# A hybrid retention and RG-LRU layer on one core: the recurrence output's last blocks as a pair, norm sums from PSUM, transfers ranked by issue

## The chip, the core and the metric

The kernel runs on one core of a Trainium2 chip. Its time is the device time of one execution in microseconds; three executions of the kernel before gave 1575.84, 1577.02 and 1579.26, median 1577.02 us.

## The reference

One layer of a streaming encoder, batch 1, 1024 tokens (T), width 1024 (D), feed-forward width 3072, everything in fp32:

```python
h = rms_norm(x, norm1_w)
q, k, v, g_ret, x_lru, y_lru, gate_ret, gate_lru = split(h @ w_in)
y_a = (group_norm(retention(rotary(q), rotary(k), v)) * silu(g_ret)) @ w_ret_o
y_b = (rg_lru(conv4(x_lru)) * gelu(y_lru)) @ w_lru_o
mix = sigmoid(gate_ret + b0) * y_a + sigmoid(gate_lru + b1) * y_b
x = x + mix @ w_out
h = rms_norm(x, norm2_w)
gate, val = split(h @ w_up)
x = x + (gelu(conv3(gate)) * val) @ w_dn
return rms_norm(x, norm_f_w)
```

## The kernel before

**Matmuls.** Each operand tile (128x512, fp32) is split into a high and a low part: ScalarE casts the high part (L471), VectorE subtracts it from the source for the low part (L472). A product is the sum of three matmuls, high by high, high by low, low by high. On top of that a large matmul is done in jobs of a 2x2 block scheme with seven products where eight would be plain: `A11, S1, S2, A12, S3, A22, S4` (PRODS). Each needs its own stationary block (a sum of weight blocks, held in `w` tiles; sums at L557 to L566) and its own set of moving tiles (B11, T1, T2, B21, T3, T4, B22, held in `u` tiles). T1 to T4 are sums of blocks of the operand: T1 = B12 - B11, T2 = B22 - T1, T3 = B12 - B22, T4 = B21 - T2. A product is 12 matmuls of 128x512 into one PSUM bank (L720).

**Banks.** A job uses three banks, X, Y and Z, of a pool of six (`g`); a second pool of two (`a`) serves transposes and small sums. A11, S2, S3 and A22 follow each other in bank X, and after each of the first three ScalarE copies the bank to an SBUF tile (L769). The next product of that bank adds to it and so waits for the copy. VectorE makes the job's four results from the copies and the banks (L743, L749, L771).

**Order of the work.** TensorE's order is the order in which `mm_fast` (from L694) issues products. Two jobs that are mates run product by product: A11 of one, A11 of the other, S1 of one, and so on. A job without a mate runs its seven products in a row, except that A11 of the next job is put between its S3 and its A22 (`ahead` in `run`). The other engines' orders come from a planner (`Plan`): the program is first drafted; `latest` goes through it backwards and gives each instruction the latest time by which it should start, taking from each engine's heap the entry of the latest due time; `forward` goes through it forwards and always takes the ready instruction with the earliest such time. `landing` is the planner's own figure for how long a transfer takes. The program is then built a second time in the planned order, and each engine executes its list in order.

**Transfers.** All large DMAs but those of the feed-forward activations are issued from one queue (SP), with eight semaphores in turn, so that a DMA waits for the one that had its semaphore before.

**The stages.** Input projection with the two branches; four jobs for the retention output (w_ro, as pairs 0+1 and 2+3); four jobs for the recurrence output (w_lo: a pair 0+1, then 2 and 3 alone); four jobs for w_out (0 and 1 a pair, 2 and 3 alone); 24 jobs up, 12 down; a final norm.

The results of a recurrence output job are multiplied by their gate (L1418), added to the retention part (L1419) and written to a DRAM buffer `mix_d` (L1421). A w_out job uses `mix` as its stationary blocks: when all the parts that a block needs are written, it is read back (L523), and then cast and summed. The moving operand of w_out, `wop`, is the weight itself: its blocks are loaded from `w_out` (L1761), its sums T1 to T4, made long before, from `tw_d` (L1374). The builder of that operand is posted by `out_start` after one of the recurrence output jobs.

After w_out, each result's squares are summed on ScalarE (L1701). `norm_half` scales the rows by the reciprocal root, and transposes them on TensorE into `a` banks (L1742); for each of the eight blocks of a half it takes the high part (ScalarE, L1747), the low part (VectorE, L1748) and a plain copy (ScalarE, L1751), and releases the bank. Blocks B12, which are needed in sums only, get just the copy. In the second half the order is B22, then B12. `set_by_set` (L861 to L881) then makes T1 to T4 for the up jobs, with the sums L863, L867, L871 and L876.

Of the kernel before, what the change touches and what calls it, by code (L numbers as in the profile page):

```python
# [15 lines left out]
AF = mybir.ActivationFunctionType  # L16
ALU = mybir.AluOpType
# [70 lines left out]
LATE, SOONER = 6, 1  # L88
# [5 lines left out]
class Units:  # L94
# [25 lines left out]
    def put(self, *tiles, late=LATE):  # L120
        for t in tiles:
            self.count += 1
            heapq.heappush(self.q, (self.now[0] + late, self.count, self.at.pop(id(t))[0]))
# [76 lines left out]
class Plan:  # L200
# [54 lines left out]

    def landing(self, s):
        if s.bytes <= 4096:
            return 1950.0
        return (self.READ if s.read else self.WRITE) + s.bytes * self.MOVE

    def latest(self, pe):

        todo = {n: len(a) for n, a in self.after.items()}
        due = dict.fromkeys(self.steps, 0.0)
        free = dict.fromkeys(self.ENGINES, 0.0)
        heaps = {e: [] for e in self.ENGINES}
        start, left, open_pe = {}, len(self.steps), set()
        pe = list(pe)

        def ready(n):  # L270
            s = self.steps[n]
            if s.eng == "PE":
                open_pe.add(n)
            else:
                heapq.heappush(heaps[s.eng], (-due[n], n))

        def end(n):
            s = self.steps[n]
            return min(free[s.eng], due[n] - (self.landing(s) if s.dma else s.tail))

        for n, k in todo.items():
            if not k:
                ready(n)
        while left:
            best = None
            for e in self.ENGINES:
                if e == "PE":
                    n = pe[-1] if pe and pe[-1] in open_pe else None
                else:
                    n = heaps[e][0][1] if heaps[e] else None  # L290
                if n is not None and (best is None or end(n) > best[0]):
                    best = end(n), e, n
            t, e, n = best
            pe.pop() if e == "PE" else heapq.heappop(heaps[e])
            s = self.steps[n]
            start[n] = free[e] = t - s.hold
            left -= 1
            for a in self.before[n]:
                p = self.steps[a]
                lag = self.lag(p, s, False)  # L300
                due[a] = min(due[a], start[n] + 1e6 if lag is None else start[n] - lag)
                todo[a] -= 1
                if not todo[a]:
                    ready(a)
        return start
# [122 lines left out]
def tile_trunk_layer(ctx, tc, x, xt, positions, params, consts, normf, w_in, w_v, w_ro, w_lo,  # L428
# [39 lines left out]
    def split(src, get=get):  # L468

        hi, lo = get(F32R), get(F32R)  # L470
        S.copy(hi, src)  # L471
        V.tensor_sub(lo, src, hi.bitcast(F32))  # L472
        return hi, lo
# [346 lines left out]
    def pair_src(w, i):  # L820
        return lambda m, kh: w[i, 2 * m + kh]
# [38 lines left out]

    def set_by_set(op, b):  # L861
        for j in range(4):
            V.tensor_sub(b["B11", j], b["B12", j], b["B11", j])  # L863
            op["T1", j] = split(b["B11", j])
            yield 1.2
        for j in range(4):
            V.tensor_sub(b["B11", j], b["B22", j], b["B11", j])  # L867
            op["T2", j] = split(b["B11", j])
            yield 1.2
        for j in range(4):  # L870
            V.tensor_sub(b["B12", j], b["B12", j], b["B22", j])  # L871
            op["T3", j] = split(b["B12", j])
            put(b["B12", j], b["B22", j], late=SOONER)
            yield 1.2
        for j in range(4):
            V.tensor_sub(b["B21", j], b["B21", j], b["B11", j])  # L876
            op["T4", j] = split(b["B21", j])
            put(b["B21", j], b["B11", j], late=SOONER)
            yield 1.2
# [782 lines left out]
        ojobs.append(Job(pair_src(w_ro, n), og, emit_ret_o(n), u_start if n == 1 else None, fast=True, last=n == 3,  # L1662
                         mate=n in (0, 2), fetch=from_sg(0, n), rate=RO_RATE))
    for n in range(4):
        ojobs.append(Job(pair_src(w_lo, n), u, emit_lru_o(n), fast=True, last=n == 3, mate=n == 0,
                         fetch=from_sg_t1(n)))
    jobs += ojobs
    warmth = get()
# [50 lines left out]
    def norm_half(half):  # L1719
# [18 lines left out]
        for k in (range(KT), (4, 5, 6, 7, 0, 1, 2, 3))[half]:  # L1738
            ps = psa.get()
            for t in range(4):  # L1740
                c0 = 128 * (k % 4)
                PE.transpose(ps[:, 128 * t:128 * t + 128], z[t, k // 4][:, c0:c0 + 128], ident)  # L1742
            w = pc("norm2_w", k)
            key = f"B{k // 4 + 1}{half + 1}", k % 4
            if key[0] != "B12":
                hi, lo = get(F32R), get(F32R)
                S.activation(hi, ps, AF.Copy, scale=w)  # L1747
                V.scalar_tensor_tensor(lo, ps, w, hi.bitcast(F32), ALU.mult, ALU.subtract)  # L1748
                h2[key] = (hi, lo)
            f = keep2[key] = get()  # L1750
            S.activation(f, ps, AF.Copy, scale=w)  # L1751
            psa.put(ps)
            yield (0.5, 0.25)[half]
        put(*z.values())
# [9 lines left out]
    def out_start():  # L1764
# [4 lines left out]
                 pre=((0, 0), (0, 1), (1, 1)), fetch=from_x(t), mate=t == 0, prods=FIRST if t < 2 else PRODS,  # L1769
                 ready=lambda m, kh, t=t: all((4 * kh + j, t // 2) in mixed for j in range(4)))  # L1770
             for t in range(4)]
    ojobs[-2].post = out_start
    queue.extend(wjobs)

    run(jobs)
# [257 lines left out]
```

## Time and profile before

| what | value |
|---|---|
| median of three runs | 1577.02 us (1575.84 to 1579.26) |
| profiled execution, its own time | 1576.54 us |
| its span in the profile | 1574.8 us |
| granted TensorE clock, mean | 0.999 |
| TensorE busy | 1561.6 us, 99% of the span |
| VectorE busy | 1382.9 us, 88% |
| ScalarE busy | 954.1 us, 61% |
| DMA, whole span | 281.07 MB, mean 178 GB/s |
| matmuls, of which L720 | 7061, 6060 |

The span is what the profile records between the first and the last instruction; the execution's own time is 1.7 us longer. PE is TensorE's matmuls, ACT ScalarE, DVE VectorE, SP the queue that issues transfers. Where an engine is busy for 99% of the span, the interesting rows are those of its idle time: which instruction came late, and what ended the wait. A row of a timeline ends with that in brackets.

### The profile page before, as it was taken

Reading aid. Unit: us, or ns where it says so; the run is one execution under the profiler, and the core shown is the slowest. Engines: PE = TensorE matmul, PEld = TensorE weight load, DVE = VectorE, ACT = ScalarE, POOL = GpSimd, SP = SyncE. Lnnn points to the kernel's source line nnn. Section 1 sums busy time; section 2 is a strip of 40 time slices with the busy share of each in tenths; the row PEclk is TensorE's granted clock in tenths of the full one; section 3 lists DMA queues with packets and bytes.
Section 4 is the critical chain, followed back from the end, with each engine's and each line's share of the span. In section 5 each row is a group of like instructions: output and inputs, shape, how many; then the busy total and the mean of one; then the engine's idle time right before and its main releaser. Section 6 shows DMA issues by size and latency. Waiting matters only on the chain.

```text
span 1574.8 us, 21660 instructions
## 1 busy us (share of the span) xinstructions
PE 1561.6 (99%) x7061; PEld 1289.4 (82%) x7061; DVE 1382.9 (88%) x2472; ACT 954.1 (61%) x1655; POOL 63.3 (4%) x81
## 2 busy tenths in 40 slices
PE   9999999999999999999999999999999999999998
PEld 7888888888878888888878888888888888888887
DVE  8999988988989998999998899777777778987885
ACT  7547966656558797855365764444444446563653
POOL 0001000000000000000000001000000000000000
PEclk9999999999999999999999999999999999999999
DMA  9344333454364346684997246444444466787752
GB/s 313 110 134 146 127 126 115 137 193 143 112 205 141 114 140 189 224 278 156 309 336 241 86 134 208 138 144 140 135 140 138 138 192 223 261 277 268 262 181 85
DMA packets 158865, 281.07 MB, mean 178 GB/s; under 512 B 17304, under 2 KB 29728, under 8 KB 158752
## 3 DMA queue, kind: packets, MB, share of 16 engines
q1 hardware_dynamic: 152944, 263.43, 51.2%
q0 software_dynamic: 4224, 13.64, 2.9%
q10 hardware_dynamic: 1584, 2.63, 0.5%
q8 instruction: 55, 0.90, 0.2%
q14 instruction: 58, 0.48, 0.1%
HBM read 194.68 MB, written 83.89 MB: 177 GB/s over the span
## 4 chain that ended last, share of the span: by engine, by line
PE 45%; DVE 4%; DMA 2%; issue 1%; ACT 1%; SPq 0%; POOLq 0%; DVEq 0%; ACTq 0%
PE g L720 44%; DVE w L472 1%; DVE u L472 1%; DMA mix_d<-u 1%; DVE u L1419 0%; PE a L1742 0%; DMA u<-sg_d 0%; DMA w<-mix_d 0%; DMA x_d<-u 0%; DVE u L749 0%; DVE u L1418 0%; DMA u<-x 0%; DMA u<-w_out 0%; DVE w L560 0%; DVE w L563 0%
## 5 line engine op out<-in xcount | busy, mean ns | idle before, releaser
L720 PE MATMUL g<-u,w 128*128 128x512 f32 x6060 | 1414.7, 391 | 4.1 <-ACT u L769 2.5
L720 PEld LDWEIGHTS g<-u,w 128*128 128x128 f32 x6060 | 1129.2, 188 | 236.0 <-ACT u L769 4.5
L471 ACT CAST w<-w 128x512 fp32r<-128x512 f32 x519 | 317.9, 621 | 324.1 <-PE g L720 222.6
L472 DVE TENSOR_TENSOR w<-w,w 128x512 fp32r<-128x512 f32 x519 | 351.7, 683 | 54.4 <-ACT w L471 49.2
L749 DVE TENSOR_TENSOR u<-g,u 128x512 f32<-128x512 f32 x216 | 147.3, 684 | 45.8 <-PE g L720 35.4
L471 ACT CAST u<-u 128x512 fp32r<-128x512 f32 x253 | 150.3, 620 | 55.2 <-PE g L720 5.3
L769 ACT COPY u<-g 128x512 f32<-128x512 f32 x218 | 126.8, 582 | 79.8 <-PE g L720 72.9
L472 DVE TENSOR_TENSOR u<-u,u 128x512 fp32r<-128x512 f32 x253 | 166.4, 682 | 1.4 <-ACT u L471 1.2
L1789 DVE SCALAR_TENSOR_TENSOR u<-u,par,u 128x511 f32<-128x511 f32 (+1 forms) x96 | 71.3, 745 | 2.9 <-ACT u L1786 2.6
L1472 PE MATMUL g<-w,u 128*128 128x512 f32 x264 | 61.9, 390 | 0.2
L1472 PEld LDWEIGHTS g<-w,u 128*128 128x128 f32 x264 | 49.3, 188 | 11.6 <-issue 0.7
L557 DVE TENSOR_TENSOR w<-w,w 128x512 f32<-128x512 f32 x72 | 49.2, 684 | 6.1 <-DMA w<-ff_d 2.2
L1794 POOL DMA_DIRECT2D ff_d<-u x48 | 36.1, 753 | 450.3 <-DVE u L1793 450.3
L1124 PE MATMUL a<-u,u 128*128 128x512 f32 x192 | 50.8, 391 | 0.1
L560 DVE TENSOR_TENSOR w<-w,w 128x512 f32<-128x512 f32 x72 | 49.2, 684 | 0.8
L563 DVE TENSOR_TENSOR w<-w,w 128x512 f32<-128x512 f32 x72 | 49.1, 683 | 0.2
L566 DVE TENSOR_TENSOR w<-w,w 128x512 f32<-128x512 f32 x72 | 49.1, 682 | 0.1
L1786 ACT ACTIVATE u<-u,par 128x512 f32<-128x512 f32 x48 | 39.2, 818 | 15.1 <-DVE u L749 14.6
L743 DVE TENSOR_TENSOR u<-u,u 128x512 f32<-128x512 f32 x48 | 32.6, 686 | 16.8 <-ACT u L769 15.9
L1124 PEld LDWEIGHTS a<-u,u 128*128 128x128 f32 x192 | 35.6, 188 | 8.8 <-ACT u L471 0.8
L1793 DVE TENSOR_TENSOR u<-u,u 128x512 f32<-128x512 f32 x48 | 32.9, 687 | 6.0 <-ACT u L1792 5.8
L1106 DVE SCALAR_TENSOR_TENSOR u<-u,par,u 128x511 f32<-128x511 f32 (+2 forms) x48 | 35.7, 743 | 0.7 <-ACT u L1102 0.6
(207 smaller groups left out, 1114.8 us busy)
## 6 DMA issues: line engine op xcount, KB each, us to landing
w<-w_in SPq DMA_DIRECT2D x96, 256.0 KB, 2.8
w<-w_up SPq DMA_DIRECT2D x96, 256.0 KB, 2.8
u<-w_dn SPq DMA_DIRECT2D x84, 256.0 KB, 3.6
u<-x_d SPq DMA_DIRECT2D x60, 256.0 KB, 4.5
x_d<-u SPq DMA_DIRECT2D x48, 256.0 KB, 3.8
ff_d<-u POOLq DMA_DIRECT2D x48, 256.0 KB, 2.7
td_d<-u SPq DMA_DIRECT2D x48, 256.0 KB, 2.8
u<-td_d SPq DMA_DIRECT2D x48, 256.0 KB, 4.6
```

The lines of the kernel that those rows point to most:

```text
L471: S.copy(hi, src)
L472: V.tensor_sub(lo, src, hi.bitcast(F32))
L557: V.tensor_add(s, r["A21"], r["A22"])
L560: V.tensor_sub(s, s, r["A11"])
L563: V.tensor_sub(s, r["A12"], s)
L566: V.tensor_sub(src, r["A21"], r["A11"])
L720: PE.matmul(bank[:, s], w[a][:, c], need(op, (SETS[nm], j))[b][:, s], start=first and n == 0, stop=n == 11, skip_group_check=True)
L749: V.tensor_add(u, bank, u)
L769: S.copy(u, bank)
L1124: PE.matmul(ps, wg[g][a][:, cs], xs[k][b], start=q == 0, stop=q == 5)
L1472: PE.matmul(bank, o[p][:, c], w[q], start=first and j == n == 0, stop=j == 3 and n == 2, skip_group_check=True)
L1789: V.scalar_tensor_tensor(c[:, s:], src[:, :TH - s], w, c[:, s:], ALU.mult, ALU.add)
```

## The change

Six edits. (1) Recurrence output jobs 2 and 3 become mates, so that the last half of that output runs as a pair, product by product. (2) `out_start`, and with it the loads of the w_out operand, is posted by the third from last of the eight output jobs (`ojobs[-3]`, recurrence block 1), not by the second from last (block 2). (3) For the blocks B12 of the norm, VectorE makes B12 - B11 and B12 - B22 straight from the PSUM bank, scaled by the norm's weight; ScalarE's copy of these blocks goes, and so do the two subtractions of `set_by_set`. (4) There B22 is released after T2. (5) The planner's figure for transfers of up to 4096 bytes goes from 1950 to 4000. (6) The planner's backward pass takes from a heap the entry with the latest due time for its issue: the due time less the transfer's landing, or less an instruction's tail.

```diff
     def landing(self, s):
         if s.bytes <= 4096:
-            return 1950.0
+            return 4000.0
...
-                heapq.heappush(heaps[s.eng], (-due[n], n))
+                heapq.heappush(heaps[s.eng], (-due[n] + (self.landing(s) if s.dma else s.tail), n))
...
     def set_by_set(op, b):
         for j in range(4):
-            V.tensor_sub(b["B11", j], b["B12", j], b["B11", j])
             op["T1", j] = split(b["B11", j])
             yield 1.2
         for j in range(4):
             V.tensor_sub(b["B11", j], b["B22", j], b["B11", j])
             op["T2", j] = split(b["B11", j])
+            put(b["B22", j], late=SOONER)
             yield 1.2
         for j in range(4):
-            V.tensor_sub(b["B12", j], b["B12", j], b["B22", j])
             op["T3", j] = split(b["B12", j])
-            put(b["B12", j], b["B22", j], late=SOONER)
+            put(b["B12", j], late=SOONER)
             yield 1.2
...
-        ojobs.append(Job(pair_src(w_lo, n), u, emit_lru_o(n), fast=True, last=n == 3, mate=n == 0,
+        ojobs.append(Job(pair_src(w_lo, n), u, emit_lru_o(n), fast=True, last=n == 3, mate=n in (0, 2),
...
             f = keep2[key] = get()
-            S.activation(f, ps, AF.Copy, scale=w)
+            if key[0] != "B12":
+                S.activation(f, ps, AF.Copy, scale=w)
+            else:
+                b11, b22 = keep2["B11", key[1]], keep2["B22", key[1]]
+                V.scalar_tensor_tensor(b11, ps, w, b11, ALU.mult, ALU.subtract)
+                V.scalar_tensor_tensor(f, ps, w, b22, ALU.mult, ALU.subtract)
             psa.put(ps)
...
-    ojobs[-2].post = out_start
+    ojobs[-3].post = out_start
```

**TensorE, the last job of the recurrence output.** Before: the end of S3 of job 3 (bank g_223), seven matmuls of A11 of w_out's first job (bank g_231), and the first matmuls of A22 of job 3.

```order
L720 MATMUL g_223_8000<-u_1380_7528,w_1331_7990 128x512
L720 MATMUL g_223_8000<-u_1379_7527,w_1332_7991 128x512
L720 MATMUL g_231_8322<-u_1522_8149,w_1351_8061 128x512
L720 MATMUL g_231_8322<-u_1523_8150,w_1351_8061 128x512
L720 MATMUL g_231_8322<-u_1522_8149,w_1352_8062 128x512
L720 MATMUL g_231_8322<-u_1526_8155,w_1351_8061 128x512
L720 MATMUL g_231_8322<-u_1527_8156,w_1351_8061 128x512
L720 MATMUL g_231_8322<-u_1526_8155,w_1352_8062 128x512
L720 MATMUL g_231_8322<-u_1530_8161,w_1351_8061 128x512
L720 MATMUL g_223_8000<-u_1382_7532,w_1338_8015 128x512
L720 MATMUL g_223_8000<-u_1383_7533,w_1338_8015 128x512
```

Now: the end of S3 of job 3 (bank g_220) and the beginning of A22 of job 2 (bank g_219), whose S3 is the twelve matmuls ahead of these of g_220.

```order
L720 MATMUL g_220_7899<-u_1379_7527,w_1321_7968 128x512
L720 MATMUL g_220_7899<-u_1380_7528,w_1321_7968 128x512
L720 MATMUL g_220_7899<-u_1379_7527,w_1322_7969 128x512
L720 MATMUL g_219_7878<-u_1382_7532,w_1325_7972 128x512
L720 MATMUL g_219_7878<-u_1383_7533,w_1325_7972 128x512
L720 MATMUL g_219_7878<-u_1382_7532,w_1326_7973 128x512
```

A product of the mate now stands between a bank's S3 and A22 (12 matmuls, and 36 between S2 and S3, where 12 were). From the end of job 3's A22 to the first matmul of A12 of w_out's first job there are now 72 matmuls, before 53.

**VectorE, the last gate product that w_out's first job waits for.** Before: L1418 with bank g_223 and the sum L1419, rows 1377 and 1378 of VectorE's list, behind five splits (L472) of the w_out operand; the list is shown from row 1371.

```order
L749 TENSOR_TENSOR u_1567_8217<-g_226_8069,u_1567_8217 128x512
L472 TENSOR_TENSOR u_1582_8240<-u_1525_8153,u_1581_8239 128x512
L472 TENSOR_TENSOR u_1586_8246<-u_1529_8159,u_1585_8245 128x512
L472 TENSOR_TENSOR u_1590_8252<-u_1533_8165,u_1589_8251 128x512
L472 TENSOR_TENSOR u_1612_8301<-u_1558_8203,u_1611_8300 128x512
L472 TENSOR_TENSOR u_1616_8307<-u_1562_8209,u_1615_8306 128x512
L1418 TENSOR_TENSOR u_1545_8183<-g_223_8000,u_1545_8183 128x512
L1419 TENSOR_TENSOR u_1544_8181<-u_1544_8181,u_1545_8183 128x512
```

Now, from row 1366 (the new lines put L1418 and L1419 at L1417 and L1418): the same for job 2 (bank g_219), then job 3 (bank g_220).

```order
L1417 TENSOR_TENSOR u_1548_8134<-g_219_7878,u_1548_8134 128x512
L472 TENSOR_TENSOR w_1367_8223<-w_1365_8220,w_1366_8222 128x512
L1418 TENSOR_TENSOR u_1547_8132<-u_1547_8132,u_1548_8134 128x512
L472 TENSOR_TENSOR u_1538_8119<-u_1470_7926,u_1537_8118 128x512
L472 TENSOR_TENSOR u_1551_8155<-u_1487_7986,u_1550_8154 128x512
L1417 TENSOR_TENSOR u_1562_8172<-g_220_7899,u_1562_8172 128x512
L1418 TENSOR_TENSOR u_1561_8170<-u_1561_8170,u_1562_8172 128x512
L472 TENSOR_TENSOR u_1632_8331<-u_1571_8192,u_1631_8330 128x512
```

The last gate product and its sum have moved from rows 1377 and 1378 to 1371 and 1372; two splits of the w_out operand, not five, stand just ahead of them.

**ScalarE and VectorE, the last blocks of the norm and the start of the up jobs.** Before, on ScalarE, rows 989 to 999: the four copies L1751 of B12 (from banks a_391 to a_397) between copies of product banks (L769) and casts of the first T1 tiles (L471).

```order
L1747 ACTIVATE u_1838_9243<-a_389_9238,par 128x512
L1751 ACTIVATE u_1837_9236<-a_387_9227,par 128x512
L1751 ACTIVATE u_1840_9247<-a_389_9238,par 128x512
L1751 ACTIVATE u_1842_9274<-a_391_9269,par 128x512
L769 COPY u_1860_9364<-g_261_9327 128x512
L1751 ACTIVATE u_1843_9281<-a_393_9276,par 128x512
L471 CAST u_1854_9350<-u_1756_8991 128x512
L1751 ACTIVATE u_1844_9288<-a_395_9283,par 128x512
L769 COPY u_1865_9397<-g_262_9366 128x512
L1751 ACTIVATE u_1845_9295<-a_397_9290,par 128x512
L471 CAST u_1856_9355<-u_1759_9002 128x512
```

Now, on VectorE, rows 1525 to 1534: the sums L1754 (B12 - B11, into B11's tile) and L1755 (B12 - B22) from the same four banks, in place of L863 and L871.

```order
L1754 SCALAR_TENSOR_TENSOR u_1756_8991<-a_391_9269,par,u_1756_8991 128x512
L566 TENSOR_TENSOR w_1491_8829<-w_1524_9023,w_1491_8829 128x512
L1754 SCALAR_TENSOR_TENSOR u_1759_9002<-a_393_9277,par,u_1759_9002 128x512
L1755 SCALAR_TENSOR_TENSOR u_1842_9274<-a_391_9269,par,u_1831_9214 128x512
L1755 SCALAR_TENSOR_TENSOR u_1843_9282<-a_393_9277,par,u_1834_9225 128x512
L472 TENSOR_TENSOR u_1855_9354<-u_1756_8991,u_1854_9353 128x512
L472 TENSOR_TENSOR u_1857_9358<-u_1759_9002,u_1856_9357 128x512
L1754 SCALAR_TENSOR_TENSOR u_1772_9042<-a_395_9285,par,u_1772_9042 128x512
L1754 SCALAR_TENSOR_TENSOR u_1775_9053<-a_397_9293,par,u_1775_9053 128x512
L866 TENSOR_TENSOR u_1756_8991<-u_1831_9214,u_1756_8991 128x512
```

The four copies are gone from ScalarE's list, and a bank is now read twice by VectorE; for the last two banks (a_395, a_397) the second read, L1755, is at rows 1545 and 1546.

## The prediction

> **What bounds the kernel now.** I read the page's head first, then TensorE's waits, then the timelines of the engines around each wait, and the chain last.
>
> ```profile
> span 1574.8 us, 21660 instructions
> PE 1561.6 (99%) x7061; PEld 1289.4 (82%) x7061; DVE 1382.9 (88%) x2472; ACT 954.1 (61%) x1655; POOL 63.3 (4%) x81
> PE g L720 <- ACT u L769: 2.5, 4, 1.3
> PE g L720 <- ACT w L471: 1.3, 1, 1.3
> PE a L1742 <- ACT a L1701: 0.5, 1, 0.5
> PE g L720 <- ACT u L471: 0.3, 1, 0.3
> 900.57 664.90 PE g L720 x2932
> ```
>
> TensorE (PE) is busy for 99% of the span, and the change leaves its matmuls as they are, in number and shape. The last row, from the chain of waits, says that from 900.57 us on they run without a gap: 664.90/2932 = 0.2268 us each. So time is to be had only from PE's waits ahead of 900, which the rows above it list (total, times, longest). They total some 5 us: a few tenths of a per cent of the span are all that this change can win. PE's timeline shows where they stand (start, length, count, in brackets the idle time before the row and what ended it):
>
> ```profile
> 764.61 20.11 PE L720 MATMUL g<-u,w 128*128 128x512 f32 x88
> 785.45 4.62 PE L720 MATMUL g<-u,w 128*128 128x512 f32 x19 [0.72 <-ACT u L769]
> 791.40 15.03 PE L720 MATMUL g<-u,w 128*128 128x512 f32 x65 [1.33 <-ACT u L769]
> 807.70 17.53 PE L720 MATMUL g<-u,w 128*128 128x512 f32 x75 [1.28 <-ACT w L471]
> 857.00 0.66 PE L1742 MATMUL a<-cst,u 128*128 128x128 f32 x4 [0.48 <-ACT a L1701]
> 898.44 1.88 PE L720 MATMUL g<-u,w 128*128 128x512 f32 x7 [0.25 <-ACT u L769]
> 900.57 11.63 PE L720 MATMUL g<-u,w 128*128 128x512 f32 x50 [0.26 <-ACT u L471]
> ```
>
> A row's length holds 0.16 us in which the next matmul could already run (88 x 0.2268 = 19.96, the row says 20.11), so each wait costs its idle time and 0.16: **0.88, 1.49 and 1.44** in the last half of the recurrence output and at the start of w_out, then 0.64, 0.41 and 0.42 around the norm. Six waits, 5.3 us.
>
> The first two are waits for the copy of bank X (L769). ScalarE's own timeline shows why the copy is late:
>
> ```profile
> 783.59 0.62 ACT L471 CAST u<-u 128x512 fp32r<-128x512 f32 x1 [1.55 <-DMA u<-w_out]
> 784.29 0.62 ACT L471 CAST w<-w 128x512 fp32r<-128x512 f32 x1
> 784.81 0.58 ACT L769 COPY u<-g 128x512 f32<-128x512 f32 x1
> ...
> 789.61 1.25 ACT L471 CAST u<-u 128x512 fp32r<-128x512 f32 x2 [0.63 <-DMA u<-tw_d]
> 790.76 0.58 ACT L769 COPY u<-g 128x512 f32<-128x512 f32 x1
> 780.00:810.00 30.00, 26.67 (x114) 20.82 (x113) 27.87 (x46) 20.51 (x37) 0.00 (x0) 1.00 1.06 376
> ```
>
> Both copies stand in ScalarE's order behind casts of the w_out operand, which wait for their transfers. The last row (busy time of PE, weight loads, DVE, ACT, POOL; then clock, DMA share, GB/s) shows the DMA engines full at 1.06 and VectorE 27.87 of 30 us busy: here everything but PE is short. The third wait is the chain:
>
> ```profile
> 795.35 0.68 DVE L1418 TENSOR_TENSOR u<-g,u 128x512 f32<-128x512 f32 x1
> 796.06 0.70 DVE u L1419
> 796.78 4.80 DMA mix_d<-u
> 801.65 0.32 SPq L523
> 802.49 5.21 DMA w<-mix_d
> 807.72 0.63 ACT w L471
> ```
>
> The last tile that w_out's first job needs is gated (L1418, L1419), written to DRAM, read back as a stationary block, cast. From the write's issue to the first matmul of that product (A12 of job 0) it takes 807.70 - 796.78 = 10.92 us.
>
> **The change, part by part.** *The pair.* The diff makes recurrence output blocks 2 and 3 a pair. Before, the single job had 7 matmuls between S3 and A22 of one bank, 7 x 0.2268 = 1.59 us for a copy that takes 0.58 and stands behind others; between S2 and S3 there were 12. Now 12 of the mate stand between S3 and A22 (2.72 us) and 36 between S2 and S3 (8.2 us). Both waits were at most 1.49 with the shorter cover. The S2-S3 one is then covered by 24 further matmuls (5.4 us), the S3-A22 one by 5 more (1.13 us): 0.88 and 1.49 go, though the copies of the pair still stand behind casts of the w_out operand in ScalarE's order. Value -2.37, ends 0 (both return, below) and -2.37.
>
> What is late next is the chain. Without the two waits PE would be at job 0's A12 at 807.70 - 1.44 - 2.37 = 803.89; the last A22 moves from 53 to 72 matmuls ahead of it, 19 x 0.2268 = 4.3 us earlier, and is through at about 803.89 - 72 x 0.2268 = 787.6. But VectorE does not come to it then, being full:
>
> ```profile
> 791.74 0.68 DVE L749 TENSOR_TENSOR u<-g,u 128x512 f32<-128x512 f32 x1
> 792.34 3.09 DVE L472 TENSOR_TENSOR u<-u,u 128x512 fp32r<-128x512 f32 x5
> ```
>
> In VectorE's order of the changed kernel the last gate product and sum are rows 1371 and 1372, before 1377 and 1378; the rows that had these six places were the one at 791.74 and the five from 792.34. So the sum ends near 793.0 and the write goes at about 793.1. Plus 10.92: 804.0 against 803.89, a wait of 0.1. With a busier DMA queue, and VectorE ahead or behind by two instructions (0.60 us from start to start in its row of five: 3.09 = 4 x 0.60 + 0.69), I hold 0 to 1.5 possible and take 0.6. So the third wait shrinks by 0.84.
>
> *The norm's sums.* Four copies L1751 and the subtractions L863 and L871 (4 each) go; eight VectorE sums straight from PSUM come.
>
> ```profile
> L1751 ACT ACTIVATE u<-a,par 128x512 f32<-128x512 f32 x16 | 10.9, 691 | 2.3 <-DVE u L1748 2.0 <-PE a L1742 0.3
> L863 DVE TENSOR_TENSOR u<-u,u 128x512 f32<-128x512 f32 x4 | 2.7, 686 | 1.8 <-ACT u L1751 1.8
> L1748 DVE SCALAR_TENSOR_TENSOR u<-a,par,u 128x512 fp32r<-128x512 f32 x12 | 8.8, 746 | 1.6 <-ACT u L1747 1.6
> 896.11 0.70 ACT L1751 ACTIVATE u<-a,par 128x512 f32<-128x512 f32 x1
> 896.69 0.63 ACT L471 CAST u<-u 128x512 fp32r<-128x512 f32 x1
> 897.20 0.70 ACT L1751 ACTIVATE u<-a,par 128x512 f32<-128x512 f32 x1
> 897.78 0.60 ACT L769 COPY u<-g 128x512 f32<-128x512 f32 x1
> ```
>
> A VectorE sum of this kind costs 746 ns (L1748 has the same operands) against 686 for what it replaces: 8 x 0.06 = 0.5 us more on VectorE. Four of them stand ahead of the first T1 split, where three subtractions stood: 0.60 + 4 x 0.06 = 0.84 us later in VectorE's order. That is hidden, since the L863 row shows 1.8 us of idle time ahead of these subtractions, waiting for the copies L1751 that the sums no longer need. ScalarE loses 4 x 0.69 = 2.8 us, and it was back to back there: the copy that ended the wait at 898.44 stood behind three of them, and the cast that ended the one at 900.57 behind the last. Both waits (0.41 + 0.42) go; what can come instead is a wait of the last two transposes for their PSUM bank, which is now held by two VectorE sums (1.5 us) rather than one 0.69 copy. I take 0.2 for that: -0.63, ends -0.83 and +0.8 (two banks, 1.49 - 0.69 = 0.8 each, less 0.83).
>
> [...]
>
> ```profile
> L749 DVE TENSOR_TENSOR u<-g,u 128x512 f32<-128x512 f32 x216 | 147.3, 684 | 45.8 <-PE g L720 35.4 <-ACT u L769 10.1
> L743 DVE TENSOR_TENSOR u<-u,u 128x512 f32<-128x512 f32 x48 | 32.6, 686 | 16.8 <-ACT u L769 15.9 <-DMA u<-x 0.7
> ```
>
> [...]
>
> *Transfers ranked by issue, small ones due earlier, the operand started one job earlier.* These cost no instruction but one more ACT table load. They reorder each engine before about 900 us: PE's rows move by at most 30 places, on average by under 3. From the third up job on all engines' orders are the same as before, so nothing happens after 900.57. PE had waits of about 2.2 us in total before 700; reordering may remove some or add as many.
>
> ```profile
> L1147 ACT ACT_TABLE_LOAD x13 | 16.7, 1283 | 0.2
> 150.00:460.00 310.00, 309.44 (x1523) 258.89 (x1522) 283.46 (x583) 206.07 (x390) 11.30 (x8) 1.00 0.43 140
> ```
>
> The table load (1.28 us) falls where ScalarE has a third of its time free (206 of 310 us busy). I take 0, ends -1 and +1.5 (a table load that no idle time covers).
>
> Sum: -2.37 - 0.84 - 0.63 + 0 = **-3.84 us**. The profiled execution took 1576.54 (its span is 1574.8), so 1572.7; the median of the three runs stands 0.48 above the profiled one: **1573.2**.
>
> **The rivals.** *The waits only move.* If the last sum does not come earlier (VectorE as late as 796.06, since its order there is set by splits whose casts wait for transfers), PE arrives at A12 at 803.89 and waits until 807.70, 3.8 us: the gain of the pair is nil, and -0.63 remains: 1576.4. For it speaks the full DMA queue (1.06); against it the six places in VectorE's order, and that the first w_out load stands ten places earlier in SP's.
>
> *Slower.* The loads of the w_out operand now start a job earlier, and two splits of that operand stand just ahead of the last gate product in VectorE's row (1369, 1370). If their transfers are late, the product waits behind them in order, and with it the write, the read and A12. To come out 3.15 us above the median of before, the wait at A12 must be 3.15 + 3.81 + 0.63 = 7.6 us, the write at 800.6, 7.5 later than I put it. One that is at 801 gives 1580.6. Against it: the longest transfer on the chain in this stretch is below, and those loads are issued ten or more places before.
>
> ```profile
> 780.11 5.49 DMA mix_d<-u
> ```
>
> *Reordering.* Keys that rank transfers by issue might expose a wait in the projections or the values stage: +1.3 where one table load comes onto the path and up to +3 where two such delays coincide, or the 2.2 us of old waits go: 1571.0 to 1576.2.
>
> **How the numbers follow.** A difference under 0.2% (3.15 us) can't be told from none in this kernel. The sum lies 0.7 us beyond that bound, so the chances split: forecast 0.62 (0.46 of it faster, 0.16 within), waits only move 0.18 (0.17 within, 0.01 slower), slower by late loads 0.10, reordering 0.10 (half faster, half within). Together faster 0.51, same 0.38, slower 0.11. The range: low by the residual wait gone (-0.6), old waits gone (-1) and the norm's last tenths (-0.2): 1571.4, rounded to 1571.2; high where the waits only move and one term of 1 us goes wrong: 1577.4.
>
> **What would show it.** In the changed kernel's PE timeline there is no wait for L769 in the stretch from 780 to 795; one wait for an L471 cast near 804 of under 1.5 us; the last mix_d write ahead of w_out's first reads is issued near 793; the waits at 898 and 900 are replaced by at most a short one for VectorE's L1755 or L1754; the last gap-free piece still lasts 664.9 us and starts near 896.7. A write at 796 or later, or a wait for L769 that is back, makes me wrong.

## The result, and the profile after

The changed kernel took 1572.97 us (median of 9 runs, 1571.51 to 1573.98), the kernel before 1577.02 (9 runs): a ratio of 0.9973, 95% interval 0.9963 to 0.9983. The forecast was 1573.2. The time is right; the terms of the sum behind it are not all right, and that their errors cancel is luck, as the rest of this document shows.

The page's head and TensorE's waits, after:

```profile
span 1570.8 us, 21640 instructions
PE 1559.6 (99%) x7061; PEld 1291.1 (82%) x7061; DVE 1382.7 (88%) x2472; ACT 951.6 (61%) x1652; POOL 63.2 (4%) x81
PE g L720 <- ACT u L769: 1.1, 2, 0.9
PE a L1741 <- ACT a L1700: 0.9, 1, 0.9
PE g L1471 <- DVE u L1456: 0.8, 1, 0.8
```

The waits for L471 are gone from the list, and those for L769 went from four (2.5 us) to two (1.1). The last row is a wait of 0.81 us at 6.74, in the input projection, where the kernel before has none. Where the others stand, by TensorE's timeline (three windows):

```profile
764.67 60.68 PE L720 MATMUL g<-u,w 128*128 128x512 f32 x267
...
846.91 5.08 PE L720 MATMUL g<-u,w 128*128 128x512 f32 x21 [0.24 <-ACT u L769]
852.93 0.66 PE L1741 MATMUL a<-cst,u 128*128 128x128 f32 x4 [0.95 <-ACT a L1700]
...
893.03 513.67 PE L720 MATMUL g<-u,w 128*128 128x512 f32 x2265
1407.56 156.84 PE L720 MATMUL g<-u,w 128*128 128x512 f32 x702 [0.85 <-ACT u L769]
```

The three waits at 785, 791 and 807 are gone to the last tenth: one row of 60.68 us covers the whole stretch (267 x 0.2268 + 0.16 = 60.7). The two waits at 898 and 900 are gone as well. On the other side, the wait ahead of the first transpose, 0.48 before, is 0.95; there is a new one of 0.24 at 846.91, and one of 0.85 at 1407.56, far behind the last place at which the two kernels' orders differ.

VectorE and SP at the gate product that w_out waits for, after:

```profile
787.54 0.68 DVE L1417 TENSOR_TENSOR u<-g,u 128x512 f32<-128x512 f32 x1
788.25 0.69 DVE L1418 TENSOR_TENSOR u<-u,u 128x512 f32<-128x512 f32 x1
...
788.98 0.37 SPq L1420 DMA_DIRECT2D mix_d<-u  x1
...
793.95 0.32 SPq L523 DMA_DIRECT2D w<-mix_d  x1
```

The last write that w_out's first job needs goes at 788.98 (796.78 before), and the first read that waits for it at 793.95 (801.65 before). Around it nothing else became less busy; DMA is as full as before (1.04, before 1.06) and VectorE too (28.50 of 30 us, before 27.87), only TensorE has no hole left:

```profile
780.00:810.00 30.00, 30.00 (x134) 24.85 (x133) 28.50 (x48) 20.61 (x38) 0.00 (x0) 1.00 1.04 374
```

**Where the time went.** TensorE has 7061 matmul records in both traces, so that the time between two of them can be compared by their number. The table has, in us, the first matmul to the 3450th (the projections, the values, most of the output jobs), 3450 to 3780 less the 74.79 us that these take where nothing waits (the three waits of before lie here), 3780 to 4200 (w_out's last jobs, the norm, the first up jobs), and 4200 to 7060 (up and down). All profiled executions of this study are in it.

| kernel | to 3450 | lost in 3450-3780 | 3780-4200 | 4200-7060 | median, us | its before |
|---|---|---|---|---|---|---|
| before | 751.59 | 4.48 | 89.92 | 645.81 | 1577.02 | |
| changed | 750.98 | 0.00 | 89.95 | 646.96 | 1572.97 | 1577.02 |
| changed, second time (again) | 751.14 | 0.00 | 89.29 | 647.05 | 1572.63 | 1576.99 |
| pair | 752.05 | 0.27 | 89.63 | 646.86 | 1572.57 | 1576.57 |
| pair, earlier start (pair_post) | 752.30 | 1.57 | 90.69 | 645.86 | 1574.29 | 1576.57 |
| earlier start (post) | 752.89 | 4.80 | 89.22 | 646.53 | 1578.40 | 1576.57 |
| planner's numbers (plan) | 751.60 | 2.51 | 89.47 | 645.80 | 1574.14 | 1576.57 |
| norm's sums (norm) | 751.50 | 4.00 | 89.50 | 645.90 | 1575.49 | 1576.37 |
| all but the pair (no_pair) | 751.61 | 5.01 | 88.55 | 646.08 | 1575.35 | 1576.99 |
| all but the norm (no_norm) | 752.24 | 0.00 | 90.33 | 646.46 | 1572.70 | 1576.37 |
| all but the earlier start (no_post) | 751.56 | 0.00 | 88.95 | 646.49 | 1571.18 | 1576.37 |
| pair, ranking (pair_key) | 752.21 | 0.64 | 89.53 | 645.92 | 1573.06 | 1576.99 |
| pair, planner's numbers (pair_plan) | 750.58 | 0.00 | 88.33 | 645.88 | 1570.76 | 1576.37 |
| the same again (pair_plan2) | 751.50 | 0.31 | 89.46 | 646.10 | 1571.58 | 1576.99 |

For the changed kernel: -0.61 - 4.48 + 0.03 + 1.15 = -3.91, against a span that is 4.0 shorter. The 4.48 is more than the 3.81 of the three waits as the prediction counted them. The rows of before say why: 19 matmuls from 785.45 should take 18 x 0.2268 + 0.39 = 4.47 us (0.39 is the length of one record, by the page) and take 4.62, the 65 from 791.40 take 15.03 instead of 14.91, the 75 from 807.70 take 17.53 instead of 17.17. The three stretches after these waits thus ran 0.12 to 0.36 us longer than their count says, together 0.63, and the waits cost that beside their idle time. By the starts of single matmuls, the first after each of them was followed by the next after 0.34 us and not 0.23, and after the third wait so were the first three (0.34 to 0.35).

The pairs of equal kernels show what one profile can't tell. The stretch to matmul 3450 came out at 750.98 and 751.14, and at 750.58 and 751.50; that at the norm at 89.95 and 89.29, and at 88.33 and 89.46; the 0.85 at 1407.56 was not there the second time, but one of 0.88 at 1483.29. So differences of under about 1 us in these three columns are not read as effects below; the column of the three waits is steady to 0.3.

### The profile page after: what moved, and what is told of

The parts are those of the page before. It is cut to its first block, busy times and chain, and to the rows that moved or that the text cites. A ratio compares the mean times of both kernels' runs of the same rounds, so it can differ in the third digit from the quotient of the medians.

```text
span 1570.8 us, 21640 instructions
## 1 busy us (share of the span) xinstructions
PE 1559.6 (99%) x7061; PEld 1291.1 (82%) x7061; DVE 1382.7 (88%) x2472; ACT 951.6 (61%) x1652; POOL 63.2 (4%) x81
## 4 chain that ended last, share of the span: by engine, by line
PE 96%; DVE 2%; DMA 1%; issue 0%; ACT 0%; POOL 0%; POOLq 0%; ACTq 0%; DVEq 0%; SPq 0%
PE g L720 85%; PE g L1471 5%; PE a L1123 3%; PE a L1248 1%; PE a L1246 1%; PE a L1258 1%; DVE w L472 0%; PE a L1741 0%; PE a L1317 0%; PE a L1238 0%; DMA w<-mix_d 0%; DMA u<-xt 0%; DVE u L749 0%; PE a L1198 0%; DVE u L472 0%
## 5 line engine op out<-in xcount | busy, mean ns | idle before, releaser
L471 ACT CAST w<-w 128x512 fp32r<-128x512 f32 x519 | 318.4, 620 | 315.3 <-PE g L720 222.0
L472 DVE TENSOR_TENSOR w<-w,w 128x512 fp32r<-128x512 f32 x519 | 352.8, 685 | 57.8 <-ACT w L471 52.7
L749 DVE TENSOR_TENSOR u<-g,u 128x512 f32<-128x512 f32 x216 | 147.6, 687 | 46.0 <-PE g L720 36.4
L471 ACT CAST u<-u 128x512 fp32r<-128x512 f32 x253 | 150.2, 619 | 53.8 <-issue 5.6
L769 ACT COPY u<-g 128x512 f32<-128x512 f32 x218 | 126.4, 581 | 85.4 <-PE g L720 85.0
L472 DVE TENSOR_TENSOR u<-u,u 128x512 fp32r<-128x512 f32 x253 | 167.2, 685 | 3.5 <-ACT u L471 2.4
L1793 DVE SCALAR_TENSOR_TENSOR u<-u,par,u 128x511 f32<-128x511 f32 (+1 forms) x96 | 71.6, 747 | 2.9 <-ACT u L1790 2.6
L1790 ACT ACTIVATE u<-u,par 128x512 f32<-128x512 f32 x48 | 39.2, 817 | 16.5 <-DVE u L749 16.3
L743 DVE TENSOR_TENSOR u<-u,u 128x512 f32<-128x512 f32 x48 | 32.6, 687 | 15.4 <-ACT u L769 15.3
```

Source lines behind the costliest of these rows:

```text
L749: V.tensor_add(u, bank, u)
L769: S.copy(u, bank)
L1793: V.scalar_tensor_tensor(c[:, s:], src[:, :TH - s], w, c[:, s:], ALU.mult, ALU.add)
```

## The experiments

Two theories. **A**, the prediction's: the pair takes the waits away, by the cover of the mate's matmuls and by the earlier last A22. **B**: the waits come from the order, since casts that wait for late loads stand ahead of the copies; ranking the transfers by issue, or starting the operand earlier, takes them away, pair or not. Each kernel below is the kernel before with some of the diff's edits. The intervals are those of the ratio to the kernel before, run on the same chip.

### The pair alone

```diff
-    ... emit_lru_o(n), fast=True, last=n == 3, mate=n == 0,
+    ... emit_lru_o(n), fast=True, last=n == 3, mate=n in (0, 2),
```

Expected:

> Only the pair; the builder of the w_out operand is posted by the second from last output job as before, which with the pair means after the pair. Theory A: the cover is there, the two waits of 0.88 and 1.49 go, but the operand's tiles T3 and B11 are prepared late, so PE waits at the start of w_out; between -2.4 and +4 us. Theory B: the same or worse, since the loads come together with the last gate products. If it is as fast as with the earlier start (-3.2 or better), the earlier start is not needed.

Measured: 1572.57 us, ratio 0.9974 (0.9963 to 0.9984), as fast as the whole change within the intervals. TensorE's timeline has no wait in 765 to 815 and one behind it:

```profile
764.61 50.75 PE L720 MATMUL g<-u,w 128*128 128x512 f32 x222
...
853.85 0.66 PE L1742 MATMUL a<-cst,u 128*128 128x128 f32 x4 [0.93 <-ACT a L1701]
```

Theory A: the pair alone takes away all but 0.27 of the 4.48 us. ScalarE's timeline shows that it does so by its cover. The two copies between S3 and A22 (at 781.61 for job 2, at 784.51 for job 3) still stand behind casts:

```profile
781.61 0.58 ACT L769 COPY u<-g 128x512 f32<-128x512 f32 x1
...
783.99 0.62 ACT L471 CAST u<-u 128x512 fp32r<-128x512 f32 x1 [1.28 <-DMA u<-tw_d]
784.51 0.58 ACT L769 COPY u<-g 128x512 f32<-128x512 f32 x1
```

By the matmul numbers they end 2.6 and 2.8 us after their products, where before the two late ones ended 3.5 and 3.0 us after theirs; the mate's 12 matmuls, 2.72 us, hide nearly all of that, and the 1.59 us of a single job would not. In the changed kernel the same two copies are not late:

```profile
779.00 0.58 ACT L769 COPY u<-g 128x512 f32<-128x512 f32 x1
...
781.42 0.59 ACT L769 COPY u<-g 128x512 f32<-128x512 f32 x1 [0.80 <-PE g L720]
```

They end 1.1 and 0.8 us after their products, and ahead of the second ScalarE stood idle until the product was done. There the order that the other edits give has already done what the cover was to do (everything but the pair, below, has no wait for L769 either); 1.59 us would have been enough for these two. Without the earlier start PE does not wait at w_out's first products either, which I had thought possible: the earlier start is not needed. The waits at 898 and 900 are gone too, without the norm's edit.

### The pair with the earlier start

```diff
+    ... mate=n in (0, 2),
-    ojobs[-2].post = out_start
+    ojobs[-3].post = out_start
```

Expected:

> Only the pair and the operand's earlier start, on the kernel before. Theory A (cover: the mate's 12 matmuls between S3 and A22, and 36 between S2 and S3, hide the copies of bank X, and the last A22 stands 72 and not 53 matmuls ahead of A12 of w_out): the waits of 0.88, 1.49 and 1.44 us at 785, 791 and 807 are gone or under 0.6 in sum, -3.2 to -3.8 us, the waits at the norm stay. Theory B (order: the two waits came from casts that stood ahead of the copies and waited for late loads, and it is the ranking of the transfers by issue that removes this): without that ranking copies still stand behind casts of late loads, at least 1.5 us of waits stay between 780 and 810, -2.3 us or less.

Measured: 1574.29 us, ratio 0.9982 (0.9974 to 0.9991), slower than the pair alone by the medians; the intervals overlap. Four waits:

```profile
783.02 22.07 PE L720 MATMUL g<-u,w 128*128 128x512 f32 x96 [0.31 <-ACT u L769]
805.43 44.47 PE L720 MATMUL g<-u,w 128*128 128x512 f32 x192 [0.35 <-ACT w L471]
850.42 5.07 PE L720 MATMUL g<-u,w 128*128 128x512 f32 x21 [0.52 <-ACT u L769]
856.45 0.66 PE L1742 MATMUL a<-cst,u 128*128 128x128 f32 x4 [0.96 <-ACT a L1701]
```

Neither theory met it. 0.66 us of waits stay between 780 and 810, nearer to A's 0.6 than to B's 1.5, and 1.57 us are lost there where 4.48 were; but the time is 2.28 under before, as B had it, and in this one execution the other columns take back 0.7 us to matmul 3450 and 0.8 at the norm, neither of them beyond what equal kernels show. The pair does its work without the ranking, and with the earlier start a part of it is missing.

### The earlier start alone

```diff
-    ojobs[-2].post = out_start
+    ojobs[-3].post = out_start
```

Expected:

> Only the earlier start of the w_out operand; blocks 2 and 3 of the recurrence output stay single. Theory A: the cover between S3 and A22 stays 7 matmuls and the copy stands in the same engine order, so waits of 1 to 3 us for L769 stay and the wait at w_out's A12 stays at 0.5 to 1.5 us: 0 with 1 us either way. Theory B: loads that start a job earlier are not late any more, no cast holds the copies, the two waits go: -1.5 to -2.4 us.

Measured: 1578.40 us, ratio 1.0009 (1.0000 to 1.0018), not faster, rather slower.

```profile
787.38 19.34 PE L720 MATMUL g<-u,w 128*128 128x512 f32 x84 [1.36 <-ACT u L769]
809.48 48.66 PE L720 MATMUL g<-u,w 128*128 128x512 f32 x213 [2.75 <-ACT w L471]
```

One of the two waits for L769 went, and the wait for mix grew from 1.28 to 2.75: 4.80 us lost in all. B as to the earlier start falls; A expected the third wait at 1.5 or less and the time within 1 us of before, and was wrong in both.

### The planner's two numbers alone

```diff
-            return 1950.0
+            return 4000.0
-                heapq.heappush(heaps[s.eng], (-due[n], n))
+                heapq.heappush(heaps[s.eng], (-due[n] + (self.landing(s) if s.dma else s.tail), n))
```

Expected:

> Only the planner's two numbers (transfers ranked by issue, small ones 4000). Theory A: the three waits between 780 and 810 stay within 1 us of their sum of 3.8, and the time is that of before within 1 us. Theory B: loads are issued ahead of their casts' places, the waits of 0.88 and 1.49 us for L769 go: -1.5 to -2.4 us.

Measured: 1574.14 us, ratio 0.9985 (0.9976 to 0.9994).

```profile
785.10 4.38 PE L720 MATMUL g<-u,w 128*128 128x512 f32 x18 [0.37 <-ACT u L769]
789.79 15.27 PE L720 MATMUL g<-u,w 128*128 128x512 f32 x66 [0.31 <-ACT u L769]
805.71 48.84 PE L720 MATMUL g<-u,w 128*128 128x512 f32 x213 [0.65 <-ACT w L471]
896.02 1.90 PE L720 MATMUL g<-u,w 128*128 128x512 f32 x7 [0.26 <-ACT u L769]
898.16 17.08 PE L720 MATMUL g<-u,w 128*128 128x512 f32 x74 [0.24 <-ACT u L471]
```

Here theory A failed, and B was half right. The two numbers cut all three waits, to 2.51 us lost, without any pair. I had valued them at nothing. Which of the two does it without the pair was not run.

### Everything but the pair

The changed kernel with `mate=n == 0` in the jobs of the recurrence output. Expected:

> The changed kernel with output blocks 2 and 3 single again. Theory A (the pair carries the gain): two or three waits between 780 and 810 are back, 2 us or more in sum, and the time is 1575 or more. Theory B (the ranking, with the earlier start and the norm's sums, does without the pair): under 1 us of waits there, 1573.5 or less.

Measured: 1575.35 us, ratio 0.9991 (0.9982 to 0.9999). One wait in the stretch, the chain that leads to it, and VectorE ahead of that:

```profile
806.82 50.25 PE L720 MATMUL g<-u,w 128*128 128x512 f32 x213 [3.01 <-ACT w L471]
...
795.56 5.29 DMA mix_d<-u
800.91 0.32 SPq L523
801.27 4.86 DMA w<-mix_d
806.15 0.63 ACT w L471
...
791.59 2.49 DVE L472 TENSOR_TENSOR u<-u,u 128x512 fp32r<-128x512 f32 x4
794.00 0.68 DVE L1417 TENSOR_TENSOR u<-g,u 128x512 f32<-128x512 f32 x1
```

Theory A has its amounts, though in one wait and not in two or three. This run tells the pair's two roles apart. The order alone takes both waits for L769 away, as B says, and in this stretch nothing is won by it: PE comes to A12 sooner and waits 3.01 us for mix, 5.01 lost in all. From the write's issue to the first matmul it is 806.82 - 795.56 = 11.26 us, and with the gate product and its sum (L1417 began at 794.00) 12.8. The single job leaves 54 matmuls here, 12.2 us, between the end of its last A22 and A12. By the matmul numbers that A22 ended at 791.4, and VectorE, busy with splits, came to the gate product 2.6 us later: that is most of the wait, and a VectorE that is free at once would still have left some 0.6 of it. The pair leaves 72 matmuls, 16.3 us, enough for the 12.8 and a VectorE that is 3.5 us late. That is the rival "the waits only move" as the prediction has it, met in a kernel without the pair.

### The norm's sums alone, and everything but them

The hunks on `set_by_set` and `norm_half` alone, and the changed kernel without these two. Expected of the first:

> Only the two kinds of sums from PSUM, on the kernel before. Theory A, the prediction's: ScalarE loses four back-to-back copies, the waits of 0.41 and 0.42 us at 898 and 900 go, -0.4 to -0.8 us. Theory C, from the trace after the change: the planner then places the transposes of the norm earlier in TensorE's order, and what the two waits give is taken back by a longer wait ahead of the first transpose (0.64 us before, 1.1 in the changed kernel): the two waits gone but the stretch from 840 to 905 the same within 0.3 us, and the time within 0.5 us of before, apart from the three waits between 780 and 810, which stay (3.8 us with 1 either way).

Expected of the second:

> The changed kernel with the norm's old copies and subtractions. Theory A: slower than the changed kernel by 0.4 to 0.8 us, with the waits at the up jobs' start back: 1573.4 to 1573.8 where the changed kernel has 1573.0. Theory C: the norm's edit gives nothing, within 0.3 us of the changed kernel: 1572.7 to 1573.3, and a wait of about 1 us ahead of the first transpose.

Measured: alone 1575.49 us, ratio 0.9993 (0.9984 to 1.0002); everything but them 1572.70, ratio 0.9978 (0.9970 to 0.9987), where the changed kernel has 1572.97 and 0.9973 (0.9963 to 0.9983): 0.3 us faster by the medians, 0.8 slower by the ratios, and the intervals overlap. The norm's sums alone, TensorE's timeline from 765 to 915:

```profile
784.81 4.61 PE L720 MATMUL g<-u,w 128*128 128x512 f32 x19 [0.18 <-ACT u L769]
790.75 15.03 PE L720 MATMUL g<-u,w 128*128 128x512 f32 x65 [1.33 <-ACT u L769]
807.20 48.74 PE L720 MATMUL g<-u,w 128*128 128x512 f32 x213 [1.42 <-ACT w L471]
856.67 0.66 PE L1741 MATMUL a<-cst,u 128*128 128x128 f32 x4 [0.73 <-ACT a L1700]
```

Both waits of the up jobs' start are gone and no wait for a bank came in their place, so the mechanism of the prediction is there; the wait ahead of the first transpose is 0.25 longer, and the stretch 0.42 shorter. The interval of the ratio holds 1, so that this edit alone is no gain that can be told from none. Beside the pair nothing is left: the two waits are gone without the norm's edit as well (the pair alone, above, and everything but the norm's sums, where theory A expected them back), and with the planner's numbers the kernels with and without the sums take 0.9965 and 0.9964. Theory C, that the longer wait at the transpose takes it back, was half right: the stretch and the time moved by more than it allowed (0.42 and 0.9 us), there is such a wait in most kernels without those at 898, but the two runs of equal kernels (12.31 and 13.43 us from matmul 3880 to 3940) show that it comes and goes with the execution.

### Everything but the earlier start; the pair with the planner's numbers

The changed kernel with `ojobs[-2].post = out_start`, and that without the norm's sums as well. Expected of the first:

> The changed kernel with the w_out operand posted after the pair, as the kernel before posts it. If the earlier start is what keeps the loads from coming late (the prediction's view of what is needed beside the pair): waits of 1 us or more between 780 and 810, 1574 or more. If the pair's cover is enough, as the run with the pair alone says: no wait there, 1572 to 1573.3.

Expected of the second:

> The pair and the planner's two numbers, with neither the earlier start nor the norm's sums. The pair alone took 4.0 us off before's median and the planner's numbers alone 2.4. If both act on the same three waits between 780 and 810 (3.8 us of idle time), the sum is no more than the pair alone but for what the numbers do in the first half (0 to -0.6): 1572.0 to 1573.0. If they act on different things, up to 6 us: 1570.5 to 1571.5.

Measured: 1571.18 us, ratio 0.9965 (0.9952 to 0.9977), and 1570.76, ratio 0.9964 (0.9952 to 0.9977). The second kernel's timeline has no wait of PE from 765 to 915 in this execution; its row over the three waits:

```profile
764.72 50.48 PE L720 MATMUL g<-u,w 128*128 128x512 f32 x222
```

Neither expectation for the first kernel met its time, which is below both; no wait is in the three waits' stretch, so the cover is enough. The second is 2.2 us below the changed kernel's median (1.4 by the ratios). The sum of the pair (-4.0) and the numbers (-2.4) alone would be -6.4, and -5.6 was measured, at first sight for "different things". By the table the three waits give 4.48 only once; the rest stands in the other columns, where one profile does not tell an effect from chance. So both kernels were run once more, on one chip.

### The changed kernel and the best version again; the ranking alone with the pair

Expected of the changed kernel:

> The changed kernel itself once more, beside the best version so far on the same chip. If its lead over before is a property of the kernel: 1571.5 to 1574. The wait of 1.0 us at 1407 us, in the stretch where before and after have the same order: if it belongs to the kernel it is there again; if it is an accident of one execution it is gone or elsewhere, and the span is about 1 us shorter for it.

Expected of the pair with the planner's numbers:

> The pair with the planner's two numbers once more, to be held against the changed kernel on the same chip. If the earlier start of the w_out operand costs time (in the traces 1.0 us between the operand's stage and the norm) and the norm's sums give nothing beside the pair: 1.5 to 2.5 us under the changed kernel. If the lead was chance: within 0.8 us of it.

Expected of the pair with the ranking, small transfers left at 1950:

> The pair with the transfers ranked by issue, small transfers left at 1950. If the ranking is what the planner's numbers bring beside the pair: as fast as both numbers with the pair, 1570.3 to 1571.3, and no wait ahead of the first transpose of the norm. If it is the figure for small transfers: as the pair alone, 1572 to 1573, and a wait of about 1 us ahead of the first transpose.

Measured: 1572.63 (0.9973, 0.9963 to 0.9983), 1571.58 (0.9966, 0.9954 to 0.9978), 1573.06 (0.9973, 0.9963 to 0.9984). The lead of the smaller change over the changed kernel is 1.05 us here, after 2.2 on two chips; the intervals overlap, and neither expectation, 1.5 to 2.5 or within 0.8, was met. It is the fastest version of the study, by a lead that these runs do not settle. Both have the wait at the transpose in this execution:

```profile
852.48 0.66 PE L1741 MATMUL a<-cst,u 128*128 128x128 f32 x4 [0.85 <-ACT a L1700]
```

```profile
853.14 0.66 PE L1742 MATMUL a<-cst,u 128*128 128x128 f32 x4 [0.90 <-ACT a L1701]
```

The first of these rows is the changed kernel's, the second the smaller version's. What holds over all runs is the sign of the earlier start: by the medians the time is higher with it by 1.7 us beside the pair (1574.29 against 1572.57, one chip), by 1.8 alone (1578.40 against 1576.57, one chip), by 1.9 beside the pair and the planner's numbers (1572.70 against 1570.76, one chip), and by 0.0008 of the ratio, 1.3 us, beside everything else. In each case the intervals overlap or touch. Which instructions cost it is not settled; a copy L769 is late at 846.91, 848.44 or 850.42 in three of the four executions that have both the pair and the earlier start, and in none of the others. That the ranking alone brings what both numbers bring is not shown: 1573.06 is as the pair alone.

## Why the prediction was right

**What bounds the kernel.** Right: only waits of PE ahead of 900 could go, the change won 4.0 us, and the three waits from 785 to 807 were the bulk.

**The pair.** Right in place, and the pair alone gives it by the cover that was worked out. In the changed kernel the copies were expected still to stand behind casts of the w_out operand, and they hardly waited for them; there the other edits' order would have done for the copies, and what the pair alone brings is the longer stretch between the last A22 and A12. Mis-sized by what follows a wait: 3.81 us were counted where 4.48 were lost, since the matmuls next after each of these waits ran late too (0.34 us from start to start, not 0.23).

**The third wait.** The step that failed is "a wait of 0.1", for which the sum then took 0.6, by the place of the gate product in VectorE's order, which gave a write at 793.1. The write went at 788.98 and no wait is left. In the pair alone it went at 791.97; with the 10.92 us of the chain that makes 802.9, and PE came to A12 at 804.3, so that there was room there without any lead of VectorE. Places in an order are not times: VectorE had run ahead long before. In the stretch from 690 to 730 it had idle time before and none after (the first row is before's, the second the changed kernel's):

```profile
690.00:730.00 40.00, 40.00 (x178) 33.10 (x178) 38.74 (x64) 22.33 (x39) 0.00 (x0) 1.00 0.65 223
```

```profile
690.00:730.00 40.00, 40.00 (x179) 33.12 (x178) 40.00 (x68) 23.12 (x41) 0.00 (x0) 1.00 0.67 236
```

Counted by instruction number, VectorE was 0.5 us ahead of before at its 1230th, 2.0 at its 1270th and 3.6 at its 1380th. Five waits of VectorE before, between 704 and 783 us, are absent after and make 2.3 of these 3.1 us. An engine that is full here may have had idle time earlier, and that is slack for what comes 80 us later.

**The norm's sums.** -0.63 was forecast; the stretch lost 0.03 in the one execution and gained 0.63 in the other, and the edit left out costs nothing that the runs can tell. The two waits that the step counted go with this edit alone and with the pair alone, so beside the pair the step is no cause of its own. The sums' price was right: 748 ns each where 746 was taken, and no wait for a bank. Rows of the changed kernel show what this price goes with:

```profile
L1754 DVE SCALAR_TENSOR_TENSOR u<-a,par,u 128x512 f32<-128x512 f32 x4 | 2.9, 748 | 0.0
L1793 DVE SCALAR_TENSOR_TENSOR u<-u,par,u 128x511 f32<-128x511 f32 (+1 forms) x96 | 71.6, 747 | 2.9 <-ACT u L1790 2.6
L1142 DVE SCALAR_TENSOR_TENSOR u<-u,u 128x512 f32<-128x512 f32 x16 | 11.0, 686 | 2.7 <-ACT u L1140 2.7
```

The same form took 747 ns from SBUF (L1793, at 511 and 510 elements) and 748 from PSUM (L1754, at 512). Plain sums, by two rows of the prediction, took 684 ns with a bank among their operands (L749) and 686 without (L743). So the two sources differ by 1 to 2 ns in these rows. Nor did the form as such make the 60 ns over a plain sum: with a constant in the place of `par`, the operand of one value per partition, the instruction took 686 ns (L1142).

**Transfers ranked, operand started earlier.** The value 0 was the sum of two terms that are not zero: the planner's numbers alone give -2.4 us, mostly at the very waits that the pair removes anyway, and the earlier start costs 1.3 to 1.9 by the medians. The column to matmul 3450 moved by -0.6, less than the 0.9 by which equal kernels differ in it.

**The last piece.** It was forecast to be free of gaps, and one of 0.85 us at 1407.56, another time at 1483.29, broke it. Both times a copy L769 was late, behind casts, and ahead of these ScalarE stood idle for 1.93 and 1.97 us. The first three rows are of the first execution, the last one of the second:

```profile
1401.24 0.63 ACT L471 CAST u<-u 128x512 fp32r<-128x512 f32 x1
1403.81 1.14 ACT L471 CAST u<-u 128x512 fp32r<-128x512 f32 x2 [1.93 <-issue]
...
1406.94 0.57 ACT L769 COPY u<-g 128x512 f32<-128x512 f32 x1
```

```profile
1479.54 1.14 ACT L471 CAST u<-u 128x512 fp32r<-128x512 f32 x2 [1.97 <-DMA u<-td_d]
```

In the second the profile names a transfer. In the first it names none, but the cast at 1403.81 reads a tile that a transfer from `td_d` fills, issued at 1397.0 and landed 0.07 us ahead of the cast. Both transfers took 6.7 us to land. In the kernel before, the one at this place took 4.8 us, and PE does not wait. The place is not chance alone either: at the same matmul, number 6359, the pair alone waits 0.65 us and everything but the earlier start 0.34, with 6.5 and 5.4 us for that transfer. The order there is the same in all kernels; why the transfer takes longer in some executions stays open.

So the total, -3.84 forecast and -3.91 by the matmuls, is the -4.48 of the three waits, larger than the 3.21 of their two terms, -0.61 in the first column, which equal kernels show too, and +1.15 in the last, most of it the late transfer; the norm's -0.63 is not in it. That the totals agree to 0.1 is luck. That the pair is enough, and that the other edits together are not, is shown by two kernels: with it alone the waits are gone but for 0.27 us, and without it, with all else, they are back as one. It is not the only edit that acts on them: the planner's numbers alone take 1.97 of the 4.48.

## What to carry to other kernels

Of several waits in a row on one path, ask what the next one will be when the first are gone: here the changed kernel without its pair no longer had two of the three waits and won nothing in that stretch, because the third grew (1.28 to 3.01 us), and only the edit that also lengthened the stretch before the late read removed all three. Undo each edit by itself even where the whole is a gain: a change of six edits was matched by one of them, and another one cost time, by the medians, wherever it was tried. Read a place in an engine's list as a time only after asking how far ahead that engine may have run.

## What the runs showed of the hardware

After the waits at 785, 791 and 807 us of the kernel before, the matmuls restarted late: the stretches behind them took 0.12 to 0.36 us more than their count at 0.2268 us each, since the first matmul after each wait (the first three after the last one) was followed by the next after 0.34 to 0.35 us. On 128x512 fp32, VectorE instructions with an operand of one value per partition took some 60 ns more than those with a constant in its place: SCALAR_TENSOR_TENSOR 745 to 749 ns against 683 to 691 (696 at L944, which also writes a sum of its elements), TENSOR_SCALAR 480 to 487 against 419 to 427, in the changed kernel. Equal kernels differed from one execution to the next by waits of about 1 us at places of equal order: 0 or 0.90 us ahead of the first transpose, and 0.85 us at 1407.56 or 0.88 at 1483.29. At these two a transfer of 256 KB took 6.7 us to land; in the kernel before, the one at the first place took 4.8.
